# Two-layer hybrid transformer backbone: one conditioning load and one gate step change places

## The chip, the cores and the metric

The kernel runs on one core of one Trainium2 chip. A core has four engines that compute: TensorE (PE in the rows, with its weight loads as PEld), VectorE (DVE), ScalarE (ACT) and GpSimd (POOL). SyncE (SP) issues nearly all transfers of this kernel, on one queue that 16 DMA engines serve. The metric is the device time of one execution in microseconds (us); of several runs the median is taken.

## What is computed

The reference is a backbone of two layers over 1024 latent tokens and 256 context tokens of width 1024, in float32. Cut to what matters here:

```python
for layer in range(2):
    shift, scale, gate = split(silu(c) @ w_ada[layer] + b_ada[layer], 3)     # conditioning, latent and context
    h = rms_norm(x, norm_g[layer]) * (1 + scale) + shift
    if layer == 0:
        q, k, v, u, vv, g = split(h @ w_in0)
        q, k = rope_2d(q), rope_2d(k)
        a = windowed_sink_gqa(q, k, v, k_ctx, v_ctx, sink)   # 8 heads, 2 key heads, window 128
        b = gelu(u) * spatial(layer_norm(gelu(vv)))          # per chunk of 128 tokens, 8 groups
        y = (concat(a, b) * silu(g)) @ w_out0
    else:
        y = (latent_attention(h) * silu(g1)) @ w_out1        # 16 heads
    x = x + gate * y
return rms_norm(x, final_g)
```

The context tokens take the same path through layer 0, with a conditioning of their own.

## The kernel before

**Products.** Every float32 product is taken as three matmuls of split operands (`mm3`, lines 97 to 101): high by high (L99), high by low (L100) and low by high (L101). The high halves are made by a cast (`hi`, L87 on ScalarE, L89 on VectorE), the low halves by a subtraction (`lo`, L95, on VectorE or GpSimd). A weight block is loaded to `raw`, and becomes `w_hi` and `w_lo`; the activations are `h` (latent, one per slice of 128 channels) and `h0c` (context).

**Loads.** `load()` (L129) issues a transfer on SyncE's queue and ties it to the two loads ahead of it, so that loads keep the order in which the code asks for them. The stores of the rotated queries (L387, to `q_d`) use the same queue without that tie. A conditioning chunk `wa` has 128 x 2048 numbers (1 MB), a token tile `x` 128 x 1024 (512 KB), a weight block `raw` 512 KB.

**Stage 0** (`layer0_in`) normalises the tokens (tiles of 128: the square on ScalarE L351, the scaling on VectorE L353), transposes them on PE (L359, to `tm` and `acc`), applies scale and shift of the conditioning (`hf`, ScalarE L362), and projects keys and queries (`s`). For channel slice `c`, `ada_chunk` turns chunk `wa[c]` into that slice's scale and shift: 16 matmuls (L268), a copy on VectorE (L271), four small matmuls (L273), and two additions on VectorE (L275, L277). `ada_step` (L281) does the same for layer 1 and for the output gates (`in_w_adag`), eight chunks each, spread over the projections. The results of keys and queries are copied by ScalarE (L379, to `qk`), rotated on VectorE and GpSimd (L382 to L385), and stored (L387) or split (keys, `kh` and `kl`). In this stage a list scheduler places each engine's instructions by its model of the times, with the order of the code as input: a line that moves in the code changes places further down, too.

**Between.** The projections of the gMLP follow: for each of ten token blocks a layer norm of `z` (VectorE and GpSimd) and the spatial matmuls (L514), whose result is biased and multiplied into `u` on VectorE (L516, L518) and stored (`u_d`, L519). Then the first queries are loaded (`qf`, L687) and split to `qs`, and the first scores start (L706, L707).

**Attention of layer 0** is a generator, `attention0`, run beside another, `dense()`, which computes the gates step by step, in some 70 steps; both are written out by hand (`manual_schedule`), so that engines run in the order of the code. A table `ORDER0` gives the operations of each of 24 blocks, with four places `D` in each; at each the loop lets `dense` go on until `RATE` times the places passed is reached. The steps 1 to 3 of `dense` only put out gate 0; steps 4 to 57 are the gates 1 to 6 (nine matmuls a step, on slices of three channels), and steps 61 to 67 each take six matmuls of gate 7 and one conversion of a weight of the output projection (`load_wo`, h on L87 and L95).

The loop that the change's numbers steer:

```python
next(attention)
for _ in range(PRE):
    next(steps)
for n, _ in enumerate(attention):
    while done < (n + 1) * RATE:
        next(steps, None)
        done += 1
```

Of the kernel before, what the change touches and what calls it, by code (L numbers as in the profile page):

```python
# [25 lines left out]
EPS = 1e-6  # L26
NEG = -1e30
PTS = 3
RATE = 0.95
PRE = 3  # L30
XB = 8
ADA = ((), (), (3, 7), (3, 7), (3,))
WAB = 3
# [19 lines left out]
class Kernel:  # L53
# [257 lines left out]
    def layer0_in(self):  # L311
        nc, i = self.nc, self.i
# [26 lines left out]
        def xload(g0, gn):  # L339
            xs = []  # L340
            for j in range(gn // P):
                x = self.t(xp, [P, D], F32, "x", bufs=XB)
                load_(x, i["xs"][g0 + j * P:g0 + (j + 1) * P, :])
                xs.append(x)
            return xs
# [51 lines left out]
        def weights(j):  # L397
            return self.wblock(wp, i["w0"][8 + j], eng=("A", "G"), load=load_)
# [22 lines left out]
                    self.ada_end(b, self.ada_ps)  # L421


        xs = [xload(*GROUPS[0])]
        wa = [self.ada_load(i["w_ada0"][0])]
        ws = [weights(0)]
        wa.append(self.ada_load(i["w_ada0"][1]))
        ws.append(weights(1))
# [194 lines left out]
        with self.tc.manual_schedule(engines={E.PE, E.Activation, E.DVE, E.Pool}):  # L623
            done = 0
            attention = self.attention0(ap)
# [6 lines that stand above are left out]
# [974 lines left out]
```

## Time and profile before

| | |
|---|---|
| median of 3 runs | 1489.81 us |
| the runs | 1490.66, 1489.81, 1485.21 us |
| the profiled execution | 1485.86 us, span 1484.1 us, mean granted clock 0.995 |
| PE busy | 1419.7 us, 96% |
| VectorE, ScalarE, GpSimd busy | 884.6, 726.6, 479.2 us (60, 49, 32%) |
| transfers | 138.96 MB, mean 94 GB/s |

The profile is of one execution; its times count from the start of the span. A row of a timeline gives the start, the duration, the engine, the line, the operation and what it writes and reads; a bracket says how long the engine had been idle before it, and what ended that. Consecutive equal instructions share a row, with their number at the end. PE's matmuls are pipelined, so that the distance of two starts, not the duration of one, is what a matmul takes of PE's time.

### The profile page before, as it was taken

The page shows a single profiled execution, that of the slowest core. Times are in us where ns is not written, and L with a number is a line of the kernel's source. Part 1 is how long each engine was busy: PE and PEld are TensorE (multiplying, and loading weights), DVE is VectorE, ACT ScalarE, POOL GpSimd, SP SyncE. Part 2 cuts the span into 40 slices and gives each one's busy share as a digit, 9 for nine tenths or more (in the row PEclk, how much of TensorE's full clock was granted, in tenths as well). Part 3 has the DMA queues.
Part 4 walks back from the last instruction along what each step waited for, and adds up shares of the span by engine and source line. Part 5 has one row for each costly group of instructions (what it writes and reads, how often), then busy time and mean ns, then how long its engine had stood idle before and what let it go on. Part 6 is the DMA issues. An engine that isn't in the chain of part 4 may idle for free.

```text
span 1484.1 us, 23403 instructions
## 1 busy us (share of the span) xinstructions
PE 1419.7 (96%) x8849; PEld 1092.8 (74%) x8849; DVE 884.6 (60%) x1692; ACT 726.6 (49%) x1532; POOL 479.2 (32%) x495
## 2 busy tenths in 40 slices
PE   5999999999999699999997999999999999999997
PEld 3766899787666478879886677777777777776786
DVE  5582124346667887543663666776667667776354
ACT  4422310145656644433423666666666666677221
POOL 4343223223556642332183222132213221234100
PEclk9999999999999999999999999999999999999999
DMA  8557501222214446412132110111011111222241
GB/s 332 228 217 272 151 29 30 79 88 79 69 51 157 152 138 192 153 60 79 40 116 94 31 35 29 33 35 35 29 33 34 35 35 45 73 61 90 72 162 72
DMA packets 91465, 138.96 MB, mean 94 GB/s; under 512 B 9088, under 2 KB 67656, under 8 KB 88280
## 3 DMA queue, kind: packets, MB, share of 16 engines
q1 hardware_dynamic: 91208, 137.21, 27.8%
q8 instruction: 69, 1.13, 0.3%
q14 instruction: 44, 0.36, 0.1%
q10 hardware_dynamic: 144, 0.26, 0.0%
HBM read 105.88 MB, written 31.56 MB: 93 GB/s over the span
## 4 chain that ended last, share of the span: by engine, by line
PE 74%; DVE 8%; ACT 6%; issue 5%; DMA 4%; POOL 2%; SPq 0%; POOLq 0%; DVEq 0%; ACTq 0%
PE tm L1276 9%; PE acc L1294 7%; PE s L99 7%; PE s L100 7%; PE s L101 7%; PE b L99 5%; PE b L100 4%; PE b L101 4%; PE s L1228 4%; PE s L1229 3%; PE acc L773 2%; PE tm L99 2%; ACT prob L1266 1%; PE s L1240 1%; DVE kl L1155 1%
## 5 line engine op out<-in xcount | busy, mean ns | idle before, releaser
L1276 PE MATMUL tm<-ident,prob 128*128 128x128 f32 x1280 | 190.6, 279 | 5.1 <-DVE qa L1178 3.4
L1276 PEld LDWEIGHTS tm<-ident,prob 128*128 128x128 f32 x1280 | 141.9, 140 | 59.3 <-issue 22.8
L1283 ACT COPY pt<-tm 128x512 f32<-128x512 f32 x192 | 112.9, 588 | 137.2 <-PE tm L1276 135.6
L1251 DVE TENSOR_REDUCE peak<-s 128x1 f32<-128x1024 f32 x128 | 156.0, 1219 | 29.8 <-PE s L1240 29.1
L1266 ACT ACTIVATE prob<-s,peak 128x1024 f32<-128x1024 f32 x128 | 142.7, 1115 | 37.0 <-DVE peak L1255 34.7
L1294 PE MATMUL acc<-pt,v 128*64 128x256 f32 x1280 | 152.9, 384 | 0.1
L95 POOL TENSOR_TENSOR w_lo<-raw,w_hi 128x512 fp32r<-128x512 f32 (+1 forms) x60 | 74.3, 1251 | 172.2 <-ACT w_hi L87 85.6
L1285 DVE COPY pt<-tm 128x512 f32<-128x512 f32 x128 | 88.4, 690 | 67.2 <-PE tm L1276 65.8
L1294 PEld LDWEIGHTS acc<-pt,v 128*64 128x64 f32 x1280 | 86.4, 136 | 47.3 <-issue 6.1
L1228 PE MATMUL s<-kh,qa 128*128 128x512 f32 x256 | 112.2, 438 | 7.7 <-ACT prob L1266 6.1
L1229 PE MATMUL s<-kl,qb 128*128 128x512 f32 x256 | 101.1, 395 | 0.0
L91 POOL CAST qb<-qa 64x512 fp32r<-64x512 f32 x32 | 19.5, 611 | 190.4 <-ACT qa L1176 190.4
L99 PE MATMUL b<-h,yh 128*128 128x512 f32 x160 | 63.9, 399 | 3.9 <-ACT yh L87 2.9
L99 PE MATMUL s<-h,w_hi 128*128 128x512 f32 x160 | 63.9, 412 | 2.2 <-ACT qk L379 2.2
L100 PE MATMUL s<-h,w_hi 128*128 128x512 f32 x160 | 63.7, 398 | 0.3 <-DVE rs_v L124 0.3
L100 PE MATMUL b<-h,yh 128*128 128x512 f32 x160 | 63.3, 396 | 0.0
L101 PE MATMUL s<-h,w_lo 128*128 128x512 f32 x160 | 63.0, 395 | 0.0
L101 PE MATMUL b<-h,yl 128*128 128x512 f32 x160 | 62.4, 391 | 0.0
L1228 PEld LDWEIGHTS s<-kh,qa 128*128 128x128 f32 x256 | 48.3, 189 | 16.1 <-ACT prob L1266 9.4
L1266 ACT ACTIVATE prob<-sx,peak 128x256 f32<-128x256 f32 x128 | 60.0, 469 | 0.0
L745 DVE TENSOR_TENSOR pt<-pt,tm 128x512 f32<-128x512 f32 x68 | 42.4, 682 | 21.8 <-ACT mb L736 18.9
L751 ACT ACTIVATE pt<-pt 128x512 f32<-128x512 f32 x84 | 47.7, 625 | 13.3 <-DVE pt L745 13.3
(474 smaller groups left out, 3742.8 us busy)
## 6 DMA issues: line engine op xcount, KB each, us to landing
wa<-in_w_ada_dram SPq DMA_DIRECT2D x16, 1024.0 KB, 8.1
x<-in_xs_dram SPq DMA_DIRECT2D x20, 512.0 KB, 6.1
raw<-in_w_dram SPq DMA_DIRECT2D x17, 512.0 KB, 4.4
wa<-in_w_adag_dram SPq DMA_DIRECT2D x8, 1024.0 KB, 6.0
pe<-pe_d SPq DMA_DIRECT2D x128, 64.0 KB, 2.1
raw<-in_w_out_dram SPq DMA_DIRECT2D x10, 512.0 KB, 3.5
yf<-y_d SPq DMA_DIRECT2D x10, 512.0 KB, 6.0
x_d<-x SPq DMA_DIRECT2D x8, 512.0 KB, 4.5
```

Source lines behind the costliest of these rows:

```text
L95: e.tensor_tensor(lo, src, hi.bitcast(F32), op=ALU.subtract)
L99: mm(out, lhsT=ah, rhs=bh, start=start, stop=False)
L100: mm(out, lhsT=ah, rhs=bl, start=False, stop=False)
L101: mm(out, lhsT=al, rhs=bh, start=False, stop=stop)
L1228: mm(o, lhsT=qa[:, q], rhs=ka[:, k0:k1], start=True, stop=False)
L1229: mm(o, lhsT=qb[:, q], rhs=kb[:, k0:k1], start=False, stop=False)
L1251: nc.vector.reduce_max(m[:, 0, a:a + 1], banks[n, a], axis=AX.X)
L1266: nc.scalar.activation(probs[n][j][:, TL:T] if c else probs[n][j][:, 0:TL], src, AF.Exp, bias=peaks[n][:, 2, j:j + 1], scale=scale, accum_ ...
L1276: nc.tensor.transpose(tp[:, o * P:(o + 1) * P], probs[n][j][:, k * P:(k + 1) * P], self.ident)
L1283: nc.scalar.copy(dst, src)
L1285: nc.vector.tensor_copy(dst, src)
L1294: mm(accs[m][64 * e:64 * e + 64, 0:QG], lhsT=self.v4[hp // 2][:, kt, vc:vc + 64], rhs=pts[2 * m + e][:, kt], start=kt == 0, stop=kt == NT - 1)
```

## The change

Two numbers change, and two lines of `layer0_in` change places. `PRE` 4 lets one more step of `dense` run ahead of the loop, `RATE` 0.94 spreads the others a little thinner; `dense` is called 95 times with either, more than it has steps. The first conditioning chunk is asked for ahead of the first four token tiles.

```diff
-RATE = 0.95
-PRE = 3
+RATE = 0.94
+PRE = 4
@@ layer0_in
+        wa = [self.ada_load(i["w_ada0"][0])]
         xs = [xload(*GROUPS[0])]
-        wa = [self.ada_load(i["w_ada0"][0])]
         ws = [weights(0)]
         wa.append(self.ada_load(i["w_ada0"][1]))
```

The instructions are the same, in number and size. What stands elsewhere: SyncE's queue at the start of the program (`x` token tiles, `wa` conditioning chunks, `raw` weights; the numbers behind the names are buffers).

```order
 L129 DMA badaT<-in_badaT_dram 128x16
-L129 DMA x_156<-in_xs_dram 128x1024
+L129 DMA wa_156<-in_w_ada_dram 128x2048
 L129 DMA x_158<-in_xs_dram 128x1024
 L129 DMA x_160<-in_xs_dram 128x1024
 L129 DMA x_162<-in_xs_dram 128x1024
-L129 DMA wa_164<-in_w_ada_dram 128x2048
+L129 DMA x_164<-in_xs_dram 128x1024
 L129 DMA raw_166<-in_w_dram 128x1024
 L129 DMA wa_176<-in_w_ada_dram 128x2048
```

The chunk went ahead of the four tiles; all that follows stands where it stood.

The same queue at the end of stage 0, before (`in_w_adag` are the chunks of the output gates, `q_d` the stored queries):

```order
37 L129 DMA wa_1067<-in_w_ada_dram 128x2048
38 L129 DMA wa_1094<-in_w_adag_dram 128x2048
39 L387 DMA q_d<-qk_890 128x256
40 L387 DMA q_d<-qk_822 128x512
41 L387 DMA q_d<-qk_939 128x512
42 L387 DMA q_d<-qk_1023 128x256
43 L387 DMA q_d<-qk_984 128x512
44 L129 DMA wa_1125<-in_w_adag_dram 128x2048
45 L387 DMA q_d<-qk_1073 128x512
46 L129 DMA wa_1152<-in_w_adag_dram 128x2048
47 L129 DMA raw_1173<-in_w_dram 128x1024
```

and now:

```order
37 L129 DMA wa_1067<-in_w_ada_dram 128x2048
38 L387 DMA q_d<-qk_890 128x256
39 L387 DMA q_d<-qk_822 128x512
40 L387 DMA q_d<-qk_939 128x512
41 L387 DMA q_d<-qk_1023 128x256
42 L387 DMA q_d<-qk_984 128x512
43 L129 DMA wa_1094<-in_w_adag_dram 128x2048
44 L129 DMA wa_1125<-in_w_adag_dram 128x2048
```

The first of these chunks went behind five stores, to the place right ahead of the second chunk.

PE around the spatial matmuls of token block 8 (L514), before:

```order
1250 L99 MATMUL b_2472<-vwh,h0c 128x320
1251 L100 MATMUL b_2472<-vwl,h0c 128x320
1252 L101 MATMUL b_2472<-vwh,h0c 128x320
1253 L514 MATMUL s_2542<-wsT,z_2439 64x128 x8
1254 L99 MATMUL s_2564<-h_0_1_108,w_hi_1728 128x512
```

and now (`b_2685` is the sum of gate 1 for the first 512 tokens):

```order
1254 L101 MATMUL b_2472<-vwh,h0c 128x320
1255 L99 MATMUL b_2685<-h_0_1_108,w_hi_2556 128x512
1256 L100 MATMUL b_2685<-h_0_1_108,w_hi_2556 128x512
1257 L101 MATMUL b_2685<-h_0_1_108,w_lo_2557 128x512
1258 L99 MATMUL b_2685<-h_1_2_109,w_hi_2556 128x512
1259 L100 MATMUL b_2685<-h_1_2_109,w_hi_2556 128x512
1260 L101 MATMUL b_2685<-h_1_2_109,w_lo_2557 128x512
1261 L99 MATMUL b_2685<-h_2_3_110,w_hi_2556 128x512
1262 L100 MATMUL b_2685<-h_2_3_110,w_hi_2556 128x512
1263 L101 MATMUL b_2685<-h_2_3_110,w_lo_2557 128x512
1264 L514 MATMUL s_2542<-wsT,z_2439 64x128 x8
```

The nine matmuls of the first step of gate 1, which stood behind the first scores, went ahead of these spatial matmuls. Smaller moves beside these: on VectorE the scaling of the tenth token tile stands ahead of one cast of an h, and the bias of block 8's spatial result (L516) behind the reciprocal root of the last block's norm; on ScalarE the copy of one `qk` stands ahead of two weight casts and two key casts. From the end of the gates of layer 0 on, the order is the same on every engine.

## Rows read from the trace of the kernel before

**Rows 1.** The page's part 1, PE: busy us, share, instructions.

```profile
PE 1419.7 (96%) x8849; PEld 1092.8 (74%) x8849; DVE 884.6 (60%) x1692; ACT 726.6 (49%) x1532; POOL 479.2 (32%) x495
```

**Rows 2.** Stretches: length, busy of each engine, granted clock, DMA share, GB/s.

```profile
24.90:31.00 6.10, 5.81 (x30) 3.24 (x34) 4.62 (x19) 0.98 (x2) 1.42 (x2) 0.51 0.67 274
...
96.00:104.00 8.00, 8.00 (x48) 6.94 (x46) 7.65 (x15) 1.50 (x3) 2.34 (x3) 1.00 0.13 49
...
100.00:120.00 20.00, 20.00 (x118) 12.82 (x117) 10.87 (x21) 3.42 (x7) 9.56 (x7) 1.00 0.74 282
...
112.00:116.00 4.00, 4.00 (x33) 2.24 (x32) 2.97 (x9) 0.59 (x1) 1.79 (x1) 1.00 1.00 405
...
293.50:297.00 3.50, 3.41 (x8) 2.73 (x9) 0.95 (x2) 0.79 (x3) 0.04 (x1) 0.52 0.66 214
```

**Rows 3.** PE's waits, 20 to 130 us: us in total, times, longest.

```profile
PE acc L359 <- ACT hf L362: 3.0, 2, 2.7
PE s L99 <- ACT qk L379: 2.2, 1, 2.2
PE tm L359 <- DVE x L353: 1.0, 1, 1.0
```

**Rows 4.** Timeline of the start: start, us, engine, instruction, idle before and releaser.

```profile
13.99 0.75 DVE L353 TENSOR_SCALAR x<-x,rs_r 128x1024 f32<-128x1024 f32 x1
...
17.63 0.78 ACT L362 ACTIVATE hf<-tm,sT,aT 128x512 f32<-128x512 f32 x1 [3.03 <-DVE sT L277]
...
24.90 1.12 PE L359 MATMUL acc<-ident,x 128*128 128x128 f32 x4 [2.75 <-ACT hf L362]
```

**Rows 5.** Timeline of SyncE's queue, 87 to 107 us.

```profile
87.99 0.33 SPq L129 DMA_DIRECT2D wa<-in_w_adag_dram  x1
93.65 12.96 SPq L387 DMA_DIRECT2D q_d<-qk  x5
106.70 0.38 SPq L129 DMA_DIRECT2D wa<-in_w_adag_dram  x1
```

**Rows 6.** Timeline of the end of stage 0, 89 to 120 us.

```profile
89.55 0.85 ACT L379 COPY qk<-s 128x512 f32<-128x512 f32 x2
...
90.18 0.50 PE L99 MATMUL s<-h,w_hi 128*128 128x512 f32 x1 [2.23 <-ACT qk L379]
...
112.07 1.07 PE L281 MATMUL b<-wa,cs 128*32 128x512 f32 x8
...
116.57 1.14 ACT L87 CAST w_hi<-raw 128x512 fp32r<-128x512 f32 x2 [3.76 <-DMA raw<-in_w_dram]
...
117.27 2.53 POOL L95 TENSOR_TENSOR w_lo<-raw,w_hi 128x512 fp32r<-128x512 f32 x2 [1.82 <-ACT w_hi L87]
...
119.99 0.40 PE L101 MATMUL s<-h,w_lo 128*128 128x512 f32 x1
```

**Rows 7.** Timeline of PE up to the first scores.

```profile
275.12 0.50 PE L99 MATMUL s<-h,w_hi 128*128 128x512 f32 x1
...
280.49 0.39 PE L101 MATMUL s<-h,w_lo 128*128 128x512 f32 x1
281.45 1.09 PE L514 MATMUL s<-wsT,z 128*64 128x128 f32 x16 [0.58 <-POOL z L542]
...
293.59 0.77 PE L706 MATMUL s<-qs,kh 128*128 128x512 f32 x1 [2.51 <-POOL qs L95]
```

**Rows 8.** PE's waits, 360 to 515 us.

```profile
PE s L722 <- DVE mx L716: 5.2, 4, 2.7
...
PE tm L731 <- DVE peak L725: 2.6, 1, 2.6
```

**Rows 9.** Timeline of low halves (L95) near the attention's end.

```profile
475.64 1.22 DVE L95 TENSOR_TENSOR h<-wr,h 128x1024 fp32r<-128x1024 f32 x1 [2.22 <-ACT h L87]
...
490.20 2.16 POOL L95 TENSOR_TENSOR qs<-qf,qs 64x512 fp32r<-64x512 f32 x1
...
491.13 2.31 DVE L95 TENSOR_TENSOR h<-wr,h 128x1024 fp32r<-128x1024 f32 x1
```

## The prediction, made before the changed kernel ran

> **What bounds the kernel now.** I read the busy time of the engines first. TensorE (PE) works 1419.7 us, 96% of the span [rows 1], so only its idle time, 64 us in all, and stretches at a lower clock can be won. The change deletes no matmul and adds none: it moves work, so each term below is a wait of PE that closes, opens or moves. I then read the stretches that the two edits reach: PE's waits of the start (20 to 130 us), the stretch up to the first scores of layer 0 (274 to 297 us) and the end of that attention (470 to 510 us). Behind them, in layer 1's attention and both output stages, every engine has the same instructions in the same order, and I give that part nothing.
>
> In the start PE waits three times for more than 1 us after 20 us: 2.7 us for hf (ScalarE), 2.2 us for a rotated-key copy qk (ScalarE) and 1.0 us for the normalised token tile x (VectorE) [rows 3]. From 100 us it is busy without a gap (20.00 of 20) [rows 2]. Before the first scores it waits 2.51 us for qs [rows 7]. In the end of the attention it waits for VectorE: 5.2 us in four waits for the maxima, 2.6 us in one for peak [rows 8].
>
> **Part A: the conditioning chunk goes ahead of the four token tiles.** It is 1 MB, the tiles 0.5 MB each, and the queue moves them in the order of issue. A full queue moves 405 GB/s [rows 2], so 1.05 MB take 2.6 us, and the four tiles land 2.6 us later. What comes behind both (the first projection weights, the next chunk) has the same bytes ahead of it as before and lands when it did. The last tile was scaled at 13.99 for 0.75 us; now at about 16.6, done at 17.3. Its transpose adds some 0.5, so the first hf starts near 17.85 instead of 17.63 [rows 4]. That hf waited for the conditioning, which is now ready long before; the token tiles take its place as the late ones. The swap thus costs 0.2 us and gains nothing by itself. The second chunk's matmuls stand in front of the next transposes and start later too; I take +0.4 at 30 us, an estimate between 0 and +0.9 (the 0.2 and one tile's 0.75).
>
> The scheduler reacts to the swap further down. The scaling of the tenth token tile moves ahead of an h conversion on VectorE, so the 1.0 us wait should nearly go: −0.9, bounds −1.0 and 0. The copy of one qk moves ahead of two weight conversions and two key conversions on ScalarE. PE waited 2.2 us for just that row at 89.55 [rows 3, 6]: −2.0, bounds −2.2 and −1. Up to 104 us PE would be 2.5 us ahead.
>
> I expect this to be given back, since the same reordering moves the issue of a 1 MB load. The first chunk of the gate conditioning, issued at 87.99, goes behind the five stores of rotated queries, which SyncE issues from 93.65 to 106.6, each waiting for VectorE. The next chunk follows those stores at 106.70 [rows 5]. The load so leaves a stretch in which the DMA engines are 13% busy (96 to 104 us) and enters one where they are full (112 to 116: 1.00) [rows 2]. Everything queued behind it is up to 2.6 us later: two more chunks and the weights whose conversion starts at 116.57 on ScalarE right as they land. GpSimd makes the low halves from 117.27, 1.26 us each, so the first is there at 118.53; PE reads it first at 119.99 [rows 6]. The spare is 1.46 us against PE's old position, less for a PE that is ahead. How late these weights land depends on how early the last of the five stores goes out. If just ahead of 106.70, the lag is 2.6 and PE is 1.1 behind its old position. If 2 us earlier, the queue's idle time takes most of it (lag 0.6) and PE keeps 0.9. I take the middle, a lag of 1.5: PE reads the halves at 118.53 + 1.5 = 120.03, where it was before. **Part A: 0.0, bounds −1.4 and +1.1** (−1.4 if the lag vanishes down to the gate chunk's own use, which stood at 112.07 [rows 6]).
>
> **Part B: one more step ahead of the first scores.** The step is nine matmuls (three chunks by three products) of gate 1. It does not go into the 2.51 us wait: it stands ahead of the spatial matmuls of token block 8. From 275.12 to 280.49 the last plain projection starts 24 matmuls, one every 0.233 us [rows 7], so nine take 2.10 us. PE finished that projection 0.58 us before the spatial matmuls of block 9 could start at 281.45, since GpSimd still made their z. Now PE arrives 2.10 us later, z is where it was (VectorE's work on block 8, which waits for the shifted matmuls, fits ahead of a step that waits for GpSimd anyway), and the spatial matmuls start 1.52 us later. From there to the first scores a chain of latencies runs: bias and product on VectorE, a store, a load, conversions on ScalarE and GpSimd. It starts 1.52 us later and ends 1.52 us later, 295.1 instead of 293.59, and PE's work beside it is unchanged, so the 2.51 us stay. The step is done 2.10 us of work early, the scores come 1.52 us late: **−0.6**, bounds −0.6 and 0. After the wait the granted clock is 0.52 until 297, the lower of its two levels (1.2 GHz) [rows 2]; as the wait stays, that stays, for whatever step then stands there.
>
> **Part C: the later steps, one slot earlier.** RATE 0.94 instead of 0.95 keeps the number of calls, the first ones included (95), and moves the slots without a step from blocks 4, 9 and 14 to 4, 8, 12 and 16 of the attention. The last group of gate steps, 61 to 67, each with one conversion of an output weight on ScalarE and a low half on VectorE or GpSimd, comes one slot earlier. VectorE has no free time at the end, and one of those low halves takes it 2.31 us there against 1.22 us for the same instruction at 475.64 [rows 9]. Moving one instruction of that kind ahead of the crowded stretch relieves VectorE by 1.2 to 2.3 us, and PE waits there by more than that [rows 8]. Against it stands the missing step in block 16: six matmuls, 1.4 us of cover, of which I expect at most 0.5 to be missed. **Part C: −1.0, bounds −2.3 and +0.5.** A rule speaks against this term. The low half took 2.31 instead of 1.22 us while GpSimd ran a subtraction of its own from 490.20 to 492.36 [rows 9]. By the Trainium skill (SBUF — State Buffer, "SBUF: two separate sides") VectorE's two-input instructions and GpSimd share a port pair as an exclusive lock, so the loser waits for the whole instruction; the stretched rows agree. By that rule the moved half would be stretched in its new slot too, and C would be 0.
>
> **The sum.** 0.0 − 0.6 − 1.0 = −1.6 us. The profiled execution took 1485.86 us (span 1484.1) and becomes 1484.3. It is 0.27% below the median of the runs, 1489.81, which I take the sum from: **1488.2 us**. The bounds give −1.4 − 0.6 − 2.3 = −4.3 and +1.1 + 0 + 0.5 = +1.6, that is 1485.5 to 1491.4. The runs of before themselves lie 5.5 us apart (1485.21 to 1490.66), about 0.5% with the error of a median, and that is what a measurement of this kernel can tell from no change.
>
> **Rivals.**
> 1. *Slower, the load in the full stretch.* The gate chunk goes out just ahead of 106.70, all of 2.6 us is lost behind it, and PE waits 1.1 us beyond its old position; B gains nothing and C loses its 0.5: 1491.4. It decides once the weights of row 116.57 land later than 118.0. For it: the five stores wait for VectorE, which has hardly a gap up to there. Against: the qk that moved shortens that very chain.
> 2. *Faster, the waits stay closed.* The five stores go out early, PE keeps its 2.5 us, B 0.6 and C 2.3: 1484.4. If in addition the shorter wait at 24.90 spares the half clock behind it (5.81 us of work at 0.51 [rows 2], so 2.9 us), 1481.5.
> 3. *The change does not do what it says.* The loads gain nothing, the step fills no wait, and the end is bound by VectorE either way (with C at 0): 1489.8.
>
> **How the numbers follow.** Forecast, a gain of 1 to 3 us: 0.50. Rival 1: 0.17. Rival 2: 0.15, of which 0.05 with the clock. Rival 3: 0.18. The range reaches over the bounds and to most of rival 2, with a little on both sides for the median: 1482.5 to 1492.5. Faster by over 0.5% (under 1482.4) needs rival 2 with the clock and a lucky median: 0.07. Slower by over 0.5% (over 1497.2) has no mechanism of that price here, 0.04. Within it: 0.89.
>
> **What would show it.** Part A: the first hf at 17.8 to 18.3, released by the tile rather than the conditioning; no wait of 2.2 us near 88 to 90; the gate chunk issued near 105 to 106; a wait of PE for weights, low halves or the chunk between 109 and 121. Part B: no idle ahead of the spatial matmuls of block 9, and again about 2.5 us ahead of the first scores. Part C: less than 5.2 us in the waits for the maxima up to 515 us. Wrong would be: the stores out by 104 us, a wait ahead of the first scores under 1.5 us, or a clock of 1.0 between 25 and 31 us.

## The result, and the profile after

The kernel after took **1496.9 us** (median of 6 runs, 1494.84 to 1499.53), the kernel before 1488.77 us (median of 6, 1485.21 to 1490.66): a ratio of 1.0059, with an interval of 1.0043 to 1.0074. It is slower by 8.1 us (6.4 to 11.0 by the interval), and lies 4.4 us above the range of the prediction. The profiled execution took 1494.84 us with a span of 1493.1 us, 9.0 us more than the span before. Both profiled executions lie below the medians, that of before by 2.9 us and that of after by 2.1 us.

The start of the program, timeline of the kernel after (start, us, engine, instruction, idle before it and its releaser), which answers [rows 4]:

```profile
16.16 2.48 POOL L95 TENSOR_TENSOR w_lo<-raw,w_hi 128x512 fp32r<-128x512 f32 x2
16.22 1.21 DVE L111 SCALAR_TENSOR_TENSOR rs_w<-rs_r,rs_v 128x1 f32<-128x1 f32 x1 [0.44 <-POOL rs_r L108]
17.35 0.14 DVE L112 TENSOR_SCALAR rs_u<-rs_r 128x1 f32<-128x1 f32 x1
17.41 0.14 DVE L113 TENSOR_SCALAR rs_u<-rs_r 128x1 f32<-128x1 f32 x1
17.59 1.06 DVE L114 SCALAR_TENSOR_TENSOR rs_r<-rs_w,rs_u 128x1 f32<-128x1 f32 x1
18.68 0.75 DVE L353 TENSOR_SCALAR x<-x,rs_r 128x1024 f32<-128x1024 f32 x1
...
20.00 0.78 ACT L362 ACTIVATE hf<-tm,sT,aT 128x512 f32<-128x512 f32 x1 [5.21 <-PE tm L359]
```

The same norm and the low halves in the kernel before:

```profile
13.36 0.22 DVE L111 SCALAR_TENSOR_TENSOR rs_w<-rs_r,rs_v 128x1 f32<-128x1 f32 x1 [0.44 <-POOL rs_r L108]
...
13.73 0.22 DVE L114 SCALAR_TENSOR_TENSOR rs_r<-rs_w,rs_u 128x1 f32<-128x1 f32 x1
...
14.15 2.96 POOL L95 TENSOR_TENSOR w_lo<-raw,w_hi 128x512 fp32r<-128x512 f32 x2 [0.83 <-ACT w_hi L87]
```

The last tile came later, as said; but its norm now runs beside GpSimd's subtraction for the first weights. Before, that subtraction waited for the cast of the weights and started behind the norm's short instructions (14.15); now the weights are ready first, and it starts at 16.16, right behind the norm's own instruction on GpSimd (L108, from 15.14). Two of the norm's instructions, on 128 numbers each, take 1.21 and 1.06 us instead of 0.22, and the last scaling starts at 18.68 instead of the 16.6 that was forecast. The first hf is at 20.00 instead of 17.63, 2.4 us late.

PE's waits of the kernel after, 20 to 130 us, beside [rows 3]:

```profile
PE acc L359 <- ACT hf L362: 2.3, 1, 2.3
PE b L281 <- DMA wa<-in_w_adag_dram: 1.0, 1, 1.0
PE s L99 <- ACT qk L379: 1.0, 1, 1.0
PE b L273 <- DVE at L271: 0.8, 1, 0.8
PE s L99 <- ACT w_hi L87: 0.8, 1, 0.8
```

The wait for x is gone and the one for qk went from 2.2 to 1.0 us, as forecast in direction. New are a wait for a gate chunk (L281), one for the weights (w_hi) and one of 0.8 us for a copy of the conditioning (at). The place of the first two, timeline of SyncE's queue and then of PE and ScalarE in the kernel after, beside [rows 5, 6]:

```profile
100.34 10.33 SPq L387 DMA_DIRECT2D q_d<-qk  x5
110.75 1.04 SPq L129 DMA_DIRECT2D wa<-in_w_adag_dram  x2
...
115.59 0.44 SPq L129 DMA_DIRECT2D raw<-in_w_dram  x1
```

```profile
116.33 1.06 PE L281 MATMUL b<-wa,cs 128*32 128x512 f32 x8 [1.04 <-DMA wa<-in_w_adag_dram]
...
123.36 1.14 ACT L87 CAST w_hi<-raw 128x512 fp32r<-128x512 f32 x2 [7.41 <-DMA raw<-in_w_dram]
...
124.03 0.50 PE L99 MATMUL s<-h,w_hi 128*128 128x512 f32 x1 [0.79 <-ACT w_hi L87]
...
125.40 0.50 PE L101 MATMUL s<-h,w_lo 128*128 128x512 f32 x1
```

The five stores start 6.7 us later than before (93.65) and end 4.1 us later, and the chunk stands behind them. The group of L281 that stood at 112.07 is at 116.33, and the low halves are read at 125.40 instead of 119.99: **PE is 5.4 us behind** when the last projection of stage 0 begins.

The list of moves ahead of the prediction leaves something out: PE's and VectorE's own order in stage 0 changed too. Matched by line, operands and shape, at least 90 of the 627 PE instructions that the kernel before starts ahead of 120 us stand elsewhere, and 24 of VectorE's 185. One of these moves has a visible price. A group of chunk matmuls (L281), in the kernel before and, in two parts, in the kernel after:

```profile
85.18 2.77 PE L281 MATMUL b<-wa,cs 128*32 128x512 f32 x20
```

```profile
88.36 2.76 PE L281 MATMUL b<-wa,cs 128*32 128x512 f32 x18
...
103.40 1.04 PE L281 MATMUL b<-wa,cs 128*32 128x512 f32 x2
```

The 18 take as long as the 20 did, and the two that were split off take 1.0 us more by themselves. At the same instructions PE is 2.6 us behind at 25 us of the kernel before, 3.2 at 85, 1.9 from 90 to 101 (the shorter wait for qk), 3.0 behind the two split matmuls, 4.3 behind the wait for the chunk and 5.3 behind that for the weights.

The next place with a difference is that of the first scores. Timeline and a window behind the scores, of the kernel after (length, busy time of each engine, granted clock, DMA share, GB/s), beside [rows 2, 7]:

```profile
288.40 1.09 PE L514 MATMUL s<-wsT,z 128*64 128x128 f32 x16
...
300.44 0.50 PE L706 MATMUL s<-qs,kh 128*128 128x512 f32 x1 [2.41 <-POOL qs L95]
```

```profile
296.00:310.00 14.00, 11.59 (x59) 9.73 (x59) 4.63 (x8) 5.88 (x11) 2.55 (x2) 1.00 0.44 148
```

The spatial matmuls of block 9 (281.45 before) are 6.95 us behind, 5.4 of them from stage 0 and 1.5 from the step, and nothing is idle ahead of them. The wait ahead of the scores is there again (2.41 us), but the clock behind it is 1.00 where it was 0.52. At the attention's end, PE's waits of the kernel after, 360 to 520 us, beside [rows 8]:

```profile
PE tm L731 <- DVE peak L725: 5.3, 3, 2.6
...
PE s L722 <- DVE mx L716: 2.5, 3, 1.7
```

Of the waits for the maxima 2.7 us are gone (5.2 to 2.5), and 2.7 us more are spent on peak (2.6 to 5.3). Then the first transposes of layer 1's tail and the first scores of layer 1, in the kernel before and in the kernel after:

```profile
709.17 1.03 PE L989 MATMUL b<-ident,tok 128*128 128x128 f32 x8
...
807.70 0.47 PE L1228 MATMUL s<-kh,qa 128*128 128x512 f32 x1 [1.56 <-DVE raw L185]
```

```profile
714.35 1.03 PE L989 MATMUL b<-ident,tok 128*128 128x128 f32 x8
...
815.20 0.47 PE L1228 MATMUL s<-kh,qa 128*128 128x512 f32 x1 [1.56 <-DVE raw L185]
```

The kernel after is 5.2 us behind at 709 and 7.5 us at 808, though each engine has the same instructions in the same order there. Between, windows of the kernel before and of the kernel after:

```profile
788.00:802.00 14.00, 11.10 (x58) 9.45 (x59) 5.71 (x10) 8.38 (x17) 7.48 (x10) 1.00 0.12 39
```

```profile
788.00:802.00 14.00, 10.91 (x54) 9.58 (x53) 2.61 (x5) 6.37 (x12) 7.17 (x9) 0.76 0.39 122
```

In the kernel after, part of this stretch had the lower of the clock's two levels (1.2 GHz); in the one profile of before it had not. The experiments come back to that.

### The profile page after: what moved, and what is told of

The parts are those of the page before. It is cut to its first block, busy times and chain, and to the rows that moved or that the text cites. A ratio compares the mean times of both kernels' runs of the same rounds, so it can differ in the third digit from the quotient of the medians.

```text
span 1493.1 us, 23407 instructions
## 1 busy us (share of the span) xinstructions
PE 1427.6 (96%) x8849; PEld 1096.5 (73%) x8849; DVE 894.9 (60%) x1692; ACT 725.4 (49%) x1532; POOL 479.5 (32%) x495
## 4 chain that ended last, share of the span: by engine, by line
PE 74%; DVE 9%; ACT 7%; DMA 4%; issue 3%; POOL 2%; SPq 0%; ACTq 0%; POOLq 0%; DVEq 0%
PE tm L1276 9%; PE acc L1294 7%; PE s L99 6%; PE s L100 6%; PE s L101 6%; PE b L99 5%; PE b L101 5%; PE b L100 5%; PE s L1228 4%; PE s L1229 3%; PE acc L773 2%; ACT prob L1266 2%; PE tm L99 2%; PE s L1240 1%; DVE peak L1251 1%
## 5 line engine op out<-in xcount | busy, mean ns | idle before, releaser
L95 POOL TENSOR_TENSOR w_lo<-raw,w_hi 128x512 fp32r<-128x512 f32 (+1 forms) x60 | 73.8, 1242 | 172.6 <-ACT w_hi L87 88.2
L99 PE MATMUL b<-h,yh 128*128 128x512 f32 x160 | 63.6, 398 | 3.4 <-ACT yh L87 2.5
L99 PE MATMUL s<-h,w_hi 128*128 128x512 f32 x160 | 64.2, 414 | 2.2 <-ACT qk L379 1.0
L108 POOL TENSOR_TENSOR rs_r<-rs_v,mhalf 128x1 f32<-128x1 f32 x27 | 18.1, 669 | 110.6 <-DVE rs_v L124 110.6
```

The source lines that it names most:

```text
L95: e.tensor_tensor(lo, src, hi.bitcast(F32), op=ALU.subtract)
L99: mm(out, lhsT=ah, rhs=bh, start=start, stop=False)
```

## The experiments

Each was timed beside the kernel before on its chip, in 4 to 11 runs. All of them compute the whole result; the delay (e4) adds work to it. In the table the difference is that of the medians; the ratio and its interval come from all runs, so that the two can differ by about 1 us. As a **landmark** for stage 0 serves the first matmul on the weights of the last projection (L99), 118.73 in the kernel before:

```profile
118.73 0.50 PE L99 MATMUL s<-h,w_hi 128*128 128x512 f32 x1
```

| kernel | what differs | us more than before (ratio, interval) | landmark: us behind |
|---|---|---|---|
| after | both edits | 8.1 (1.0059, 1.0043 to 1.0074) | 5.3 |
| e7 | after once more | 6.4 (1.0049, 1.0036 to 1.0061) | 5.8 |
| e1 | loads alone | 10.7 (1.0071, 1.0059 to 1.0084) | 5.9 |
| e2 | steps alone | 0.1 (1.0000, 0.9991 to 1.0009) | −0.1 |
| e3 | after, low halves behind the norm | 2.4 (1.0020, 1.0010 to 1.0029) | 1.7 |
| e12 | e3, chunk behind the stores | 3.7 (1.0028, 1.0012 to 1.0044) | 5.7 |
| e5 | before, chunk behind the stores | 1.7 (1.0010, 1.0001 to 1.0018) | 2.4 |
| e6 | before's loads, after's order behind | 8.1 (1.0049, 1.0035 to 1.0064) | 5.0 |
| e8 | after, keys ahead of the copy | 10.8 (1.0066, 1.0048 to 1.0084) | 10.7 |
| e9 | e8, chunk behind the stores | 8.2 (1.0048, 1.0030 to 1.0067) | 10.3 |
| e10 | e3 and e8 | 3.3 (1.0018, 1.0009 to 1.0028) | 3.9 |
| e11 | after, stores behind the chunk | 5.9 (1.0051, 1.0035 to 1.0068) | 5.8 |
| e4 | before, 21 matmuls more near 740 us | 0.6 (1.0005, 0.9996 to 1.0013) | 0.3 |

**Which edit (e1, e2, e7).** The loads alone, and the two numbers alone:

```diff
+        wa = [self.ada_load(i["w_ada0"][0])]
         xs = [xload(*GROUPS[0])]
-        wa = [self.ada_load(i["w_ada0"][0])]
```

> The kernel before with the first conditioning chunk ahead of the token tiles, PRE 3 and RATE 0.95. Theory (the loads cost it): stage 0 as in the changed kernel, about +5.5 us at 140 us against before, the rest as before: 1494.3 us, or 1497 if the lower clock behind 786 us, seen in the changed kernel, comes too. Rival (the steps cost it): below +2 us, 1490.

> The kernel before with PRE 4 and RATE 0.94 alone. Theory: stage 0 as before, the step ahead of the spatial matmuls of block 8 shifts the first scores by 1.4 us for 2.1 us of work, the attention ends 0.3 to 0.7 us earlier: 1488.3 us. Rival (the steps cost it): over +3 us, 1492 or more.

> The changed kernel once more, for a second profile and for times beside the other kernels of this study. Theory (waits for chunk and weights are there in each run, lower-clock stretches differ from run to run): 1494 to 1500 us, +5 to +8 us at 140 us against before. Rival (the first measurement was off): 1492 or less.

The loads alone bring the whole loss, and the numbers alone cost and win nothing that can be measured. e2 and e7 came out as their theories said; e1, at 1498.9, is above both of its figures. It is 2.6 us slower than both edits together and 4.3 us slower than e7, with intervals that overlap the first and touch the second: whether the numbers win something once stage 0 is late is not settled. In e2's trace the first scores come 1.26 us later than before, after a wait of the same size, and the clock behind is not the lower one:

```profile
294.85 0.50 PE L706 MATMUL s<-qs,kh 128*128 128x512 f32 x1 [2.45 <-POOL qs L95]
```

```profile
295.00:299.00 4.00, 4.00 (x18) 3.29 (x19) 0.34 (x1) 0.34 (x2) 0.00 (x0) 1.00 0.62 198
```

At the transposes of 709.17 e2 is 1.0 us ahead, and at 807.70 it is 1.6 us behind: it too has a lower clock in 788 to 802 (0.76), and still its median is that of before. The profile of e2 is its median execution (1488.36), the one of before lies 2.9 us under the median. So the 2.3 us that the kernel after seems to lose there are most likely the luck of the one profile of before; no second profile of it was taken that would show this.

**The norm beside GpSimd (e3).** The low halves of the first weights get a tie behind the scaling of the fourth tile; the loads stay swapped.

```diff
+raw0 = self.raw(i["w0"][8], ...)
-ws = [weights(0)]
 norm(xs[0])
+ws = [self.wsplit(wp, raw0, behind=self.scaled), ...]
```

> The changed kernel with one more dependency: the low halves of the first weight block on GpSimd start behind the scaling of the fourth token tile. The scheduler then also puts the first gate chunk ahead of the five stores again. Theory (VectorE's short norm instructions are held up by GpSimd's subtraction): the two instructions of 1.21 and 1.06 us take 0.22 each, the first hf starts at 18.0 instead of 20.0, no wait for the gate chunk, about +1 us at 140 us against before: 1488 to 1490 us. Rival (the tiles' late landing does it): the first hf stays near 20.0, still +2.5 us at 24 us.

Timeline of e3:

```profile
16.50 0.22 DVE L111 SCALAR_TENSOR_TENSOR rs_w<-rs_r,rs_v 128x1 f32<-128x1 f32 x1 [0.44 <-POOL rs_r L108]
...
18.02 2.51 POOL L95 TENSOR_TENSOR w_lo<-raw,w_hi 128x512 fp32r<-128x512 f32 x2 [1.56 <-issue]
...
18.45 0.78 ACT L362 ACTIVATE hf<-tm,sT,aT 128x512 f32<-128x512 f32 x1 [3.45 <-PE tm L359]
```

Without the subtraction beside it the norm takes its 0.22 us again and the first hf comes 1.55 us earlier than in the kernel after (0.4 later than the theory had it; the time, 1490.6, is just above its range). That is shown. The scheduler answered this tie with moves of its own. It put the first gate chunk back ahead of the five stores, and it gave PE a third order between 23 and 104 us: at least 88 of 600 instructions stand elsewhere than in after, and the two L281 matmuls are back in their group. By 88 to 101 us e3 is only 1.0 us ahead of after. So the 5.7 us (8.1 less 2.4) that e3 wins against after belong to three things at least. The next runs price the chunk's place; no run tests PE's order by itself.

**The chunk behind the stores (e5, e12).** One tie makes the first gate chunk wait in the queue until the five stores are issued, in the kernel before (e5) and in e3 (e12). On PE, ScalarE and GpSimd the order stays as it was.

```diff
-for prev in self.loads[-2:]:
+for prev in self.loads[-2:] + ([self.stored[4]] if len(self.loads) == NL else []):
```

> The kernel before with one load moved: the first gate chunk is issued behind the five stores of rotated queries instead of ahead of them; all else stands as before. Theory (loads held behind stores that wait for VectorE cost PE the waits of 112 to 127 us): PE waits for a chunk or for weights there, +0.5 to +2.5 us at 140 us against before: 1489 to 1491 us. Rival (the late stores and the PE that is ahead make the waits, not the chunk's place): no wait, within 0.3 us at 140 us: 1488.3 us.

> The kernel whose first low halves stand behind the scaling of the fourth token tile, with the first gate chunk behind the five stores again, all else in the same order. Theory (the chunk's place costs 1 to 2 us, as it did in the kernel before): waits of PE near 112 and 120 us, 3 to 4 us behind at 120 instead of 1.95, time 1491.5 to 1493. Rival (once the start is mended the stores leave early enough): 1.95 again, time 1490 to 1491.

PE's waits of e3, 70 to 130 us, then those of e12, and e12's clock:

```profile
PE s L99 <- ACT qk L379: 0.9, 1, 0.9
PE s L99 <- ACT w_hi L87: 0.8, 1, 0.8
```

```profile
PE b L281 <- DMA wa<-in_w_adag_dram: 1.9, 1, 1.9
PE s L99 <- ACT w_hi L87: 1.0, 1, 1.0
PE s L99 <- ACT qk L379: 0.9, 1, 0.9
```

```profile
115.50:118.90 3.40, 3.40 (x18) 2.22 (x11) 0.11 (x1) 0.00 (x0) 1.23 (x1) 0.50 1.00 390
```

The move alone costs 2.1 us of waits in e12, and behind the first of them PE works 3.4 us at a clock of 0.50, 1.7 us more: 3.8 of the 4.0 us by which the landmark moved (120.47 to 124.42). In e5 the move costs a wait of 1.03 us for w_hi:

```profile
121.14 0.50 PE L99 MATMUL s<-h,w_hi 128*128 128x512 f32 x1 [1.03 <-ACT w_hi L87]
```

Of the 2.4 us behind, 1.2 were there by 90 us, in a part with unchanged order: so much can two profiles of one order differ. In time the theory of e5 held (1.7 us, 0.1 to 2.7 by the interval). So did that of e12 (1492.5), though PE is further behind than its 3 to 4 us. By the table e12 is 1.4 us over e3, which their intervals do not separate, and 4.4 us less over before than after is, with intervals that just touch. So the landmark is not the time: at nearly the same 5.3 to 5.9 us behind, e12, e11, e7, after and e1 are 3.7 to 10.7 us over before.

**The order alone (e6).** The loads as in the kernel before, and a tie that delays the second weights' low halves behind the scaling of the fifth tile. The scheduler then puts the rest of stage 0 into nearly the order of after, the chunk behind the stores included.

```diff
-ws.append(weights(1))
+raw1 = self.raw(i["w0"][9], ...)
 ...
+norm(fifth tile ...); ws.append(self.wsplit(wp, raw1, behind=self.scaled[4]))
```

> The kernel before with the low halves of the second weight block on GpSimd behind the scaling of the fifth token tile, so that the power instruction of that tile's norm no longer stands behind them. The scheduler also moves the first gate chunk behind the five stores. Theory: PE's wait of 2.75 us at 24.9 us falls to about 1 us, -1.5 us at 30 us against before; behind the chunk +0.5 to +2.5 us comes back: 1487 to 1489.5 us. Rival (the low halves are then late themselves): nothing gained at 30 us, 1490 or more.

The first hf is at 17.65, as before, and yet e6 is as slow as after. The tie itself makes PE wait 2.1 us for low halves near 24 us, so this run does not price the order cleanly. The rival of the expectation came out, and more (1496.7). The run shows that an undisturbed first norm alone does not save the time.

**Late keys (e8, e9, e10).** A reading of mine that fell. In the kernel after, ScalarE takes the copy of qk ahead of the conversions of the second keys, waits 3.71 us for its buffer, and the stores go out late. The tie puts the conversions first again; the chunk then stands ahead of the stores.

```diff
-nc.scalar.copy(d, ps[:, :gn])
+ins = nc.scalar.copy(d, ps[:, :gn])
+(j, g0) == (1, 512) and self.tc.add_manual_dep(ins.ins, self.keyhi.name, ...)
```

> The kernel after, with one tie: the copy of the second query group's rotation input (L379, qk, which waited 3.71 us at 91.46 us of the trace of after for a buffer that VectorE's key work releases) goes behind the two key conversions of the second key group (L87, kh), where the kernel before has it. The scheduler then also puts the first gate chunk back ahead of the five stores; the start is that of after. Theory (the order at the end of stage 0 costs most of the change's loss, by a blocked ScalarE that makes the stores late and by the chunk behind them): first of the five stores near 96 instead of 100.3, the weights' first read by PE within 2.5 us of before's place (119.99), time 1490.5 to 1492.5. Rival (the late start of stage 0 costs it all): still more than 4.5 us behind at 120 us, time 1494 to 1497.

> As the run with the keys ahead of the copy, but the first gate chunk behind the five stores again, as the kernel after has it. Theory (the chunk's place costs little once the stores leave early): 1 to 1.5 us more than the run with the keys alone, as where the chunk was moved in the kernel before. Rival (the chunk's place is the loss): 3 to 5 us more, the time of after.

> The kernel after with both ties: the first weights' low halves on GpSimd behind the scaling of the fourth token tile, and the copy behind the two key conversions. Theory: the start's 1.5 us and the end of stage 0 both restored, at 120 us within 1 us of the kernel before, time 1487.5 to 1490. Rival (the ties cost what they save, as the first tie left 2 us at 120 us): 1490.5, as with the first tie alone.

SyncE's queue and PE in e8, and its clock behind:

```profile
99.71 13.86 SPq L387 DMA_DIRECT2D q_d<-qk  x5
```

```profile
98.55 0.80 PE L99 MATMUL s<-h,w_hi 128*128 128x512 f32 x1 [4.87 <-ACT qk L379]
```

```profile
98.00:103.00 5.00, 4.45 (x11) 3.48 (x12) 4.81 (x8) 2.36 (x6) 2.59 (x2) 0.50 1.00 419
```

The stores left hardly earlier (99.71 against 100.34) and PE waited 4.87 us for the copy, then worked at the lower clock. So the scheduler's move of the copy does save a wait, as Part A said: taken back in the late kernel it costs 3.9 us more of waiting. The time of e8, 1499.0, is above both of its figures. Behind that wait the chunk's place costs nothing (e9, 2.6 us less than e8 where both expectations said more): PE does not wait for it. In e10 the same wait is 3.3 us, and e10, at 1491.5, wins nothing over e3, as its rival said.

**The stores behind the chunk (e11).** After's late start, with the stores tied behind the chunk.

```diff
 self.loads.append(ins.ins)
+[self.tc.add_manual_dep(s, ins.ins.name, ...) for s in (self.stored if len(self.loads) == NL + 1 else [])]
```

> The kernel after, its late start kept, with one tie: the stores of rotated queries that the program asks for ahead of the first gate chunk are queued behind it. Theory (of the 5.4 us that PE was behind at the weights of the last projection, some 3.2 come from the start and 2.2 from the chunk behind the stores): no wait of PE for a chunk or weights between 109 and 125 us, 2.5 to 3.7 us behind at 120, time 1493 to 1495.5. Rival (whatever stands ahead, the late keys alone make the weights late): again 5 us or more behind at 120, time 1496 to 1499.

PE's waits of e11, 70 to 130 us:

```profile
PE s L99 <- ACT qk L379: 2.7, 3, 1.5
```

The waits for the chunk and the weights are gone, as the theory said, and waits for copies of the same length stand in their place: the landmark is 5.8 us behind, as the rival said. The time, 5.9 us over before, is still in the theory's range. This run does not leave the late start as the only fault. SyncE's queue and two of PE's matmuls in e11:

```profile
89.16 1.19 SPq L129 DMA_DIRECT2D wa<-in_w_ada_dram  x2
98.55 0.33 SPq L129 DMA_DIRECT2D wa<-in_w_adag_dram  x1
98.93 11.99 SPq L387 DMA_DIRECT2D q_d<-qk  x5
```

```profile
97.47 1.04 PE L281 MATMUL b<-wa,cs 128*32 128x512 f32 x2
```

By the trace L281 releases the chunk: it leaves at 98.55, when the two split matmuls are done, and the stores tied behind it wait with it. In the kernel after these two end at 104.4, so the chunk could hardly have left at 87.99 there, stores or not.

**A plain delay (e4).** 21 extra matmuls on PE near 740 us, whose sums the next ones overwrite, to see whether a delay of that kind grows behind 800 us.

```diff
+[self.mm3(ps, *w[0], ..., True, True) for _ in range(7 * (j == 3 and g0 == 0))]
```

> The kernel before with 21 additional matmuls (seven times the first three products of one gate of layer 1, overwritten by the true sum) near 740 us, so that all behind them comes 4.9 us later and nothing else differs. Theory (the lower clock of 786 to 820 us hangs on when the stretch is reached): +4.9 us at 780 us and +8 us at 830 us: 1496.5 us. Rival (it hangs on what ran before, or on chance): granted clock 1.0 there, +4.9 us throughout: 1493.5 us.

Both expectations missed: of 4.9 us of added work (21 matmuls by the 0.233 us of [rows 7]) 0.6 show in the time, by its interval −0.6 to 1.9. At 786 us e4 is 4.9 us behind, at the scores of 807.70 only 1.9, and its clock in 788 to 802 was 1.00. The stretch before those scores can take in a delay. A lower clock there does not hang on the time of arrival alone: at 786 us e4, e10, e11 and after are 4.9 to 5.4 us behind, and the clock in 788 to 802 was 1.00, 1.00, 0.76 and 0.76.

## Why the prediction was wrong

**Part A is the step that failed**: forecast 0.0 (−1.4 to +1.1), measured 5.3 to 5.9 us at the landmark with the change's loads (after, e7, e1). Its start was mis-sized, its end of the stores was taken from the old program, and a new order on PE and VectorE stood in no term. Term by term:

- *The start*, +0.4 forecast, was 2.4 at the first hf and 2.6 at PE's transposes (24.90 before, 27.47 after). Of the 2.4 us e3 takes back 1.55; 0.8 remain where the later tiles were to cost 0.2. I moved the tile's scaling by the time of the transfer and left its neighbours where they were. But the weights behind the tiles landed when they did (their cast starts at 13.65, before at 13.45), so GpSimd's subtraction no longer waited for them and ran as soon as GpSimd was free, beside the norm. By the Trainium skill (SBUF — State Buffer, "SBUF: two separate sides") VectorE's instructions with two inputs and GpSimd take a shared port pair in turn, each for a whole instruction. The rows agree closely: L111 and L114, with two inputs, end at 17.43 and 18.65, the two subtractions (each half of 2.48 us from 16.16) at 17.40 and 18.64, and L112 and L113, with one input, keep their 0.14 us. I had weighed that rule in Part C and not here, where short instructions stand in a chain on which everything waits.
- *The waits for x and qk* closed by 1.0 and 1.3 us, within the bounds of the forecast (−0.9 and −2.0), and e8 shows that the copy's move saves a wait.
- *PE's order* had no term: the two split L281 matmuls cost 1.0 us and, by what e11 shows of the queue, free the chunk's buffer at 104.4 instead of 87.95. What the rest of the new order costs is open.
- *The five stores* were to end before 106.70 because the copies came earlier. They ended at 110.7, and the first went out 6.7 us late, where PE is 1.9 to 3.2 us late. The stores wait for VectorE's work on the keys; ScalarE's copy for the first store, in the kernel after:

```profile
99.94 0.37 ACT L379 COPY qk<-s 128x256 f32<-128x256 f32 x1 [3.80 <-DVE kl L95]
```

  Part of that is PE's delay. But the sum that the second keys' conversion waits for (L385) also stands behind other key work on VectorE now, at 92.36 instead of 86.50; no run takes the two apart. Rival 1 had the right mechanism, weights later than 118.0 (123.36), but its lag was bounded by the 2.6 us of one load. It took the old end of the stores for the latest one, and that was the error of the bound.

**The parts do not add up.** With start and chunk mended, and PE's order changed once more (e3), PE is 1.7 us behind and the time 2.4 us over before. With the start left (e11, where the chunk's buffer is late too) or the chunk alone (e12), PE is 5.7 to 5.8 us behind at the same place. Waits of 1 to 5 us for copies, chunk or weights take each other's place, and in e1, e8 to e10 and e12 a stretch at a clock of 0.50 (1.2 GHz) stood behind one. A split of the 5.3 us into priced causes would therefore be a story. Measured is that the loads bring the loss and that stage 0 holds most of it; that the subtraction beside the norm costs 1.55 us at the first hf (e3); and that the chunk's place costs 4.0 us at the landmark once the start is mended (e12).

**Part B** held in its mechanism: no idle ahead of the spatial matmuls, the scores 1.3 us late by e2 (1.52 forecast), the wait of 2.4 us. What I did not see is that the lower clock behind it would go. **Part C** (−1.0) cannot be told from nothing: waits moved from the maxima to peak, and e2, which has Parts B and C, is 0.1 us over before (−1.3 to 1.3), though its profile is 1.0 us ahead at 709 us. The −1.6 that both were to bring lies just outside that interval, and their lower ends together, −2.9, well outside.

**What stays open.** At 709 us the profile of after is 5.2 us behind, about what it was at the end of stage 0 (5.5 at 140 us). What the medians hold beyond that (1.2 to 5.8 us by their interval) has no cause shown: the main stretch behind it where the two profiles drift apart, 788 to 825 us (3.3 us), does so by its clock, and e2 has the same drift without being slower. Open too is what PE's and VectorE's new order in stage 0 costs by itself: e6 has nearly the order of after with the loads of before and is as slow, but its tie adds a wait of its own. No version was faster than the kernel before; e2 equals it, and e3 is its nearest with the loads swapped.

## What to carry to other kernels

When a load is moved, shift not only the work that waits for it but ask what that work now runs beside: here two 0.22 us instructions of a norm took more than 1 us each beside GpSimd's subtraction. A transfer queued behind stores leaves when their producers are done and its own buffer is free, so its bound is the latest of those times in the changed program, not the old one. Where a scheduler reorders by its own model, compare the whole order of every engine before and after, also for each repair: here the tie that mended the start changed PE's order as well, so that its gain is not the price of one fault.

## What the runs showed of the hardware

- Two VectorE instructions on 128x1 numbers took 1.21 and 1.06 us beside GpSimd's subtraction, and 0.22 us without it, in the program with that tie, where the scheduler moved other work as well.
- The clock behind the first scores of layer 0: in five profiled executions without the extra step ahead of them (before, e1, e4, e5, e6) the mean granted clock of 293 to 310 us was 0.90, after a wait of 2.45 to 2.52 us. In eight of nine with the step (after, e2, e3, e7 to e9, e11, e12; not e10) it was 1.00, after a wait of 2.41 to 2.50 us. The wait alone does not decide it. What does was not found.
- Between 788 and 808 us the granted clock differed between the profiled executions: in 788 to 802 us it was 1.00 in the profiles of before, e4 and e10, 0.76 in those of after, e7, e2 and e11, and between these in the others. The one program profiled twice (after and e7) had 0.76 both times, so program and chance are not told apart here. Comparing one profile of each kernel puts 2.3 us of it down to the change, which e2, as fast as before with the same stretch, speaks against.
